# Attention heads behind later gate banks, one tile for both heads' chunk operands and state, other fill lengths, in a two-layer hybrid decoder trunk

## The chip, the cores and the metric

The kernel runs on one core of a Trainium2 chip. Its engines are told by the names that the profile uses: PE is TensorE (matrix products; PEld is its weight loads), DVE is VectorE, ACT is ScalarE, POOL is GpSimd, SP is SyncE, which issues the transfers of the weights. The metric is the device time of one run in microseconds (us), as the median of several runs. The profile is of one further execution, whose own time stands beside it.

## The reference

Two layers over 256 tokens of width 1024. Everything is float32. Cut to what matters here:

```python
h = rmsnorm(x, norm_mix[i]);  z = h @ w_in[i]
qa, ka, va, zr, gate_a, gate_r = split(z)         # attention, RWKV, two gates
oa = diff_attention(qa, ka, va, rel_bias, lam)    # 4 heads: softmax of two maps,
                                                  # W = P1 - lam * P2, W @ v
oa = rmsnorm(oa, attn_subln[i]) * (1 - lam_init)
y_attn = oa @ w_out_attn[i]

zs = zr + (token_shift(zr) - zr) * rwkv_mu[i]     # r, k, v, decay, a, g from it
def step(state, inp):                             # 8 heads, state 64 x 64
    sa = einsum('bhvk,bhk->bhv', state, a_t)      # a = -kk,  b = kk * a
    state = state * w_t + sa[..., None] * b_t + v_t[..., None] * k_t
    return state, einsum('bhvk,bhk->bhv', state, r_t)
yr = scan(step, 0, (r, decay, k, v, -kk, kk * a))
y_rwkv = ((groupnorm(yr) + bonus) * g) @ w_out_rwkv[i]

x = x + (sigmoid(gate_a) * y_attn + sigmoid(gate_r) * y_rwkv) @ w_out[i]
x = x + (silu(h2 @ w_ffn_gate[i]) * (h2 @ w_ffn_up[i])) @ w_ffn_down[i]
x = x + sigmoid(rmsnorm(x) @ w_ple_gate[i]) * (p[i] @ w_ple[i])
```

A last rmsnorm follows. The change touches `diff_attention` and `scan` only in how they are laid out in time and in memory.

## The kernel before

**The stream.** The weights of all the large products come from HBM in loads of 512 KB (8 blocks of 128x128). For each load ScalarE makes a rounded copy `wh` (L110) and VectorE the rest `wl = raw - wh` (L111). TensorE then does three products for each block, x with wh, the rest of x with wh, and x with wl (L128 to L130; L142, L144 and L166 to L168 are the same in other shapes). This stream goes through the whole program, and the smaller work is put between its products.

**What is set between.** In each layer the input projection, the attention, the gates and the attention's output projection are one generator, `main_g`: 14 banks for RWKV (`need(b)` forces one of them to be done), then q, k, v, then 8 gate banks. In its loop over the gate banks, head b's `scores` (two products into PSUM for each of two maps, additions of the bias on VectorE L469 and L470, maxima L472 and L473, exponentials, reciprocal L479, scaling by lambda L480) comes ahead of gate bank b, and `weighted` (transposes and product with v) behind it, for b from 0 to 3. The RWKV code is written as straight steps. Between them stand calls `fill(t)`, which let `main_g` advance by about t us of stream products, and t comes from a table, FP0 for layer 0 and FP1 for layer 1, by the name of the step (`pre`, `g0`, `tr`, `q0`, ...). Both tables are the same before. A scheduler then orders the instructions of each engine.

**The RWKV steps.** The 256 tokens are 4 chunks of 64. For a chunk c and a pair j of heads (e is 0 or 1, one head on each half of the 128 partitions; `half[e]` is the half, `quar` the quarters):

- The preparation makes `NK` (two operands side by side, L668 and L670) and `RA` (two side by side, L678 and L679), `RA` once for each e and each half of the pairs, with 64 partitions filled. L712 multiplies NK with RA: 8 products for each j. From the result ScalarE copies diagonal blocks to `AT` and `L2`, and VectorE masks one part into the free half of `RA` (L722) and one into `RK` (L723).
- `SV[e]` holds the state of the head on its half of the partitions and V on the other half; `UV[e]` the corrections and V. `NT` is NK transposed (L744).
- The diagonal blocks of 32x32 are inverted on VectorE (L765 to L797), scaled by per-partition columns into `ex` (L804, L805) and transposed into `D2` (L806), once for Ds and once for Dt. `blocks` (L818) does 64 products of 32x32 with Ds, a second call 64 with Dt.
- Then the chunks in turn: L843 forms Z of both heads (8 products of 128 rows, state and masked part in one sum), L854 solves with the diagonal blocks, L861 and L871 carry it to the second half, L876 forms the state's product, and L884 and L885 update `SV`, one operation for each e. Behind chunks 1 and 3 the outputs y are formed (L898, L903) and normalised.

The program begins with 11 products of a zero tile (`NWARM`, L233), before the first weights are there.

Of the kernel before, what the change touches and what calls it, by code (L numbers as in the profile page):

```python
# [25 lines left out]
NSLOT = 27  # L26
# [4 lines left out]
NWARM = 11  # L31

FP0 = dict(pre=1.29, g0=1.05, g=0.75, vt=0.39, rk=1.13, di=1.56, su=0.7, tr=0.36, q0=2.0, q1=1.6, z=0.95, w=1.15,
          w2=0.71, u=2.27, s=1.8, gn0=8.42, gn1=10.4, s8=1.06)
FP1 = dict(pre=1.29, g0=1.05, g=0.75, vt=0.39, rk=1.13, di=1.56, su=0.7, tr=0.36, q0=2.0, q1=1.6, z=0.95, w=1.15,
          w2=0.71, u=2.27, s=1.8, gn0=8.42, gn1=10.4, s8=1.06)
# [21 lines left out]
def trunk(ctx: ExitStack, tc: tile.TileContext, x_in, p_in, ws, par, lora, cst, fin, relb, onehot, out):  # L58
# [19 lines left out]
    def slot8(shape, dt=F32, s="s8"):  # L78
        return sp.tile(shape, dt, tag="s8", bufs=1, name=nm(s))
# [287 lines left out]
    def layer(l):  # L367
# [159 lines left out]
        def main_g():  # L527
# [19 lines left out]
            side = {}  # L547
            early["lam"] = attention_lambda()
            for b in range(8):
                if b < 4:  # L550
                    side[b] = scores(b)
                    yield 1.3
                gb = gate_bank(b)
                yield from gb
                if b < 4:
                    yield from weighted(b, side[b])
                if b == 3:
                    attention_norm()
                if b == 4:
                    yield from attention_out()  # L560
            oas = [(oh_[:, k], ol_[:, k]) for k in range(4)]
# [101 lines left out]
        RA = [[slot([P, 8, P], F32, "RA") for _ in range(2)] for _ in range(2)]  # L663
        NK = slot8([P, 16, 2, 64], F32, "NK")
# [3 lines left out]
        V.scalar_tensor_tensor(out=NK[:, :, 0], in0=pt16(nb), scalar=-0.5, in1=pt16(Pi), op0=ALU.mult, op1=ALU.mult)  # L668
        fill(fp['pre'])
        V.tensor_mul(NK[:, :, 1], pt16(kp), pt16(Pi))  # L670
        fill(fp['pre'])
        for jp in range(2):
            js = slice(2 * jp, 2 * jp + 2)
            for e in range(2):
                h = half[e]
                ra = RA[e][jp]
                A.copy(ra[h, :, 0:1], pt16(kn[:, js])[h, :, 0:1])
                V.tensor_mul(ra[h, :, 1:64], pt16(kn[:, js])[h, :, 1:64], pt16(Pd[:, js])[h, :, 0:63])  # L678
                V.tensor_mul(ra[h, :, 64:128], pt16(zr[:, js])[h], pt16(Pd[:, js])[h])  # L679
                fill(fp['pre'])  # L680
# [13 lines left out]
        RK = [slot([P, 16, 64], F32, "RK") for _ in range(2)]  # L694
# [8 lines left out]
        def mask4(h, lo):  # L703
            n = h.stop - h.start
            return mg[h, lo:lo + 64].unsqueeze(1).broadcast_to([n, 4, 64])

        for j in range(4):

            pgs = [psax(), psax()]
            for c in range(4):  # L710
                for e in range(2):
                    PE.matmul(pgs[e][:, c * P:(c + 1) * P], NK[half[e], 4 * j + c].rearrange("p a s -> p (a s)"),  # L712
                              RA[e][j // 2][half[e], 4 * (j % 2) + c], start=True, stop=True)
            for e in range(2):
                h, oh = half[e], half[1 - e]
                ra = RA[e][j // 2]
                pg = pgs[e]
                pg3 = pg.rearrange("p (i s) -> p i s", i=4)
                for b in range(2):
                    A.copy(AT[quar[2 * e + b], 4 * j:4 * j + 4], pg3[quar[b], :, quar[b]])  # L720
                A.copy(L2[quar[e], 4 * j:4 * j + 4, quar[e]], pg3[0:32, :, 32:64])
# [5 lines left out]
        SV = [slot([P, 16, 64], F32, "SV") for _ in range(2)]  # L727
        UV = [slot([P, 16, 64], F32, "UV") for _ in range(2)]
        NT = [slot([P, 8, P], F32, "NT") for _ in range(2)]
        for tb in range(2):  # L730
# [4 lines left out]
            for r in range(2):  # L735
                c = 2 * tb + r
                for e in range(2):
                    A.copy(SV[e][half[1 - e], c::4], pv4[half[r], :, e])
                    A.copy(UV[e][64:128, c::4], pv4[half[r], :, e])
            fill(fp['vt'])  # L740
        for i4 in range(4):
            pn = psax()
            for i in range(4):
                PE.transpose(pn[:, i * P:(i + 1) * P], NK[:, 4 * i4 + i].rearrange("p a s -> p (a s)"), ident)  # L744
            A.copy(NT[i4 // 2][:, 4 * (i4 % 2):4 * (i4 % 2) + 4], pn.rearrange("p (i v) -> p i v", i=4))
            fill(fp['vt'])
# [84 lines left out]
        for e in range(2):  # L831
            G.memset(SV[e][half[e], 0::4], 0.0)
# [5 lines left out]
        for c in range(4):  # L838
            ch = c // 2
            pz = psax()  # L840
            for j in range(4):
# [21 lines left out]
            for e in range(2):  # L863
                G.tensor_copy(UV[e][0:32, c::4], W1[quar[e]])
# [4 lines left out]
            V.tensor_copy(UV[0][32:64, c::4], four(pw)[quar[2]])  # L869
            A.copy(UV[1][32:64, c::4], four(pw)[quar[3]])  # L870
# [363 lines left out]
```

## Time and profile before

| | |
|---|---|
| median of 3 runs | 910.44 us (908.72 to 911.51) |
| profiled execution, its own time | 909.44 us |
| its span (first to last instruction) | 907.6 us |
| mean granted clock of TensorE | 0.994 |
| PE busy | 887.8 us, 98% of the span |
| PEld (weight loads beside it) | 800.3 us, 88% |
| DVE busy | 709.6 us, 78%, 1270 instructions |
| ACT busy | 515.8 us, 57% |
| POOL busy | 18.4 us, 2% |
| chain that ended last | PE 90%, DVE 6%, ACT 2% |
| HBM read | 147.25 MB, 165 GB/s over the span |

How to read it: the chain that ended last is followed back from the last instruction to what released each; its shares say which engine's work made up the time. A busy TensorE is not TensorE at its peak, since the ends of its products are modelled: the distance from one start to the next says more than the length of one. The granted clock is the share of full speed (2.4 GHz) that the engine was given; 0.5 is the lower level of 1.2 GHz. The other engines' shares are averages over the program; a stage of its own can look different, and the windows show that. Lines as L818 are lines of the kernel before.

### The profile page before, as it was taken

What the parts mean: (1) busy time and instruction counts of PE and PEld (TensorE: products, weight loads), DVE (VectorE), ACT (ScalarE), POOL (GpSimd) and SP (SyncE); (2) the same over time, 40 slices, a digit from 0 to 9 for tenths busy, and PEclk for the clock granted to TensorE, in tenths of its full rate; (3) what the DMA queues carried; (4) which work ended last, traced back from release to release, by engine and by line L of the source; (5) the groups of instructions that cost most, each with busy time, mean ns of one, the idle gap of its engine ahead of it and who ended that gap; (6) DMA issues with size and microseconds to landing.
All of it is one profiled execution on the core that took longest, in us unless ns stands there. A gap on an engine that the chain in (4) does not pass through costs nothing.

```text
span 907.6 us, 17784 instructions
## 1 busy us (share of the span) xinstructions
PE 887.8 (98%) x7011; PEld 800.3 (88%) x7011; DVE 709.6 (78%) x1270; ACT 515.8 (57%) x956; POOL 18.4 (2%) x59
## 2 busy tenths in 40 slices
PE   8999989999999999999999999999999999999996
PEld 7988879899988888889999997989989888888885
DVE  6659977688988888766785996768788888886666
ACT  6475665544555555545567564665465555554444
POOL 0000000100000000000001000000000000000000
PEclk9999999999999999999999999999999999999998
DMA  8563423445666666666554344333665666666661
GB/s 283 190 219 131 140 75 106 126 153 165 208 186 187 188 186 190 198 186 194 170 162 136 107 135 136 95 111 105 185 188 174 195 188 187 190 201 186 192 191 47
DMA packets 42540, 149.47 MB, mean 165 GB/s; under 512 B 4911, under 2 KB 6488, under 8 KB 42328
## 3 DMA queue, kind: packets, MB, share of 16 engines
q1 hardware_dynamic: 41896, 147.87, 53.6%
q8 instruction: 55, 0.90, 0.4%
q10 hardware_dynamic: 560, 0.46, 0.2%
q14 instruction: 29, 0.24, 0.1%
HBM read 147.25 MB, written 2.63 MB: 165 GB/s over the span
## 4 chain that ended last, share of the span: by engine, by line
PE 90%; DVE 6%; ACT 2%; issue 1%; DMA 1%; ACTq 0%; POOL 0%; DVEq 0%; POOLq 0%
PE mm L142 21%; PE mm L128 11%; PE mm L144 10%; PE mm L130 10%; PE mm L129 10%; PE ax L142 8%; PE ax L144 4%; DVE wl L111 2%; ACT wh L110 1%; PE mm L166 1%; PE ax L712 1%; PE mm L167 1%; PE mm L168 1%; PE ax L818 1%; PE ax L843 1%
## 5 line engine op out<-in xcount | busy, mean ns | idle before, releaser
L110 ACT CAST wh<-raw 128x1024 fp32r<-128x1024 f32 (+1 forms) x269 | 280.7, 1046 | 297.0 <-PE mm L142 100.6
L111 DVE TENSOR_TENSOR wl<-raw,wh 128x1024 fp32r<-128x1024 f32 (+1 forms) x269 | 327.3, 1219 | 105.4 <-ACT wh L110 103.9
L128 PE MATMUL mm<-x,wh 128*128 128x256 f32 x704 | 204.1, 290 | 2.1 <-ACT wh L110 1.7
L130 PE MATMUL mm<-x,wl 128*128 128x256 f32 x704 | 202.0, 288 | 0.6 <-DVE wl L111 0.5
L129 PE MATMUL mm<-x,wh 128*128 128x256 f32 x704 | 200.6, 285 | 0.0
L128 PEld LDWEIGHTS mm<-x,wh 128*128 128x128 f32 x704 | 135.0, 192 | 6.2 <-ACT wh L110 2.2
L130 PEld LDWEIGHTS mm<-x,wl 128*128 128x128 f32 x704 | 134.9, 192 | 4.2 <-DVE wl L111 1.6
L129 PEld LDWEIGHTS mm<-x,wh 128*128 128x128 f32 x704 | 135.0, 192 | 1.1 <-issue 0.2
L142 PE MATMUL mm<-f,wh 128*128 128x512 f32 x352 | 97.5, 395 | 0.0
L142 PE MATMUL mm<-x,wh 128*128 128x512 f32 x320 | 87.5, 395 | 0.0
L142 PE MATMUL ax<-x,wh 128*128 128x512 f32 x320 | 87.3, 394 | 0.0
L142 PEld LDWEIGHTS mm<-f,wh 128*128 128x128 f32 x352 | 59.7, 189 | 7.6
L144 PEld LDWEIGHTS mm<-f,wl 128*128 128x128 f32 x352 | 55.1, 189 | 8.1
L142 PEld LDWEIGHTS ax<-x,wh 128*128 128x128 f32 x320 | 54.7, 189 | 7.3
L142 PEld LDWEIGHTS mm<-x,wh 128*128 128x128 f32 x320 | 54.7, 189 | 7.3
L144 PE MATMUL mm<-f,wl 128*128 128x256 f32 x352 | 57.2, 280 | 0.0
L144 PEld LDWEIGHTS ax<-x,wl 128*128 128x128 f32 x320 | 49.1, 189 | 6.8
L144 PEld LDWEIGHTS mm<-x,wl 128*128 128x128 f32 x320 | 49.1, 189 | 6.8
L144 PE MATMUL ax<-x,wl 128*128 128x256 f32 x320 | 50.9, 281 | 0.0
L144 PE MATMUL mm<-x,wl 128*128 128x256 f32 x320 | 50.9, 281 | 0.0
L142 PE MATMUL mm<-m,wh 128*128 128x512 f32 x128 | 35.3, 396 | 0.0
L956 DVE TENSOR_TENSOR xs<-xs,mm 128x256 f32<-128x256 f32 x64 | 26.3, 416 | 9.3 <-PE mm L144 8.7
(293 smaller groups left out, 1385.1 us busy)
## 6 DMA issues: line engine op xcount, KB each, us to landing
raw<-ws SPq DMA_DIRECT2D x267, 512.0 KB, 3.6
lora<-lora SPq DMA_DIRECT2D x2, 768.0 KB, 5.6
vr<-vd SPq DMA_DIRECT2D x1, 1536.0 KB, 9.4
bias<-vr SPq DMA_DIRECT2D x1, 1024.0 KB
out<-y SPq DMA_DIRECT2D x3, 256.0 KB, 2.1
raw<-ws SPq DMA_DIRECT2D x2, 256.0 KB, 4.6
xs<-x_in SPq DMA_DIRECT2D x1, 512.0 KB
pi<-p_in SPq DMA_DIRECT2D x2, 256.0 KB, 3.8
```

Of the source, the lines that this page charges most:

```text
L110: A.copy(wh, raw)
L111: V.tensor_sub(wl, raw, wh.bitcast(F32))
L128: PE.matmul(dst, lh, rh, start=first, stop=False, **kw)
L129: PE.matmul(dst, lh, rl, start=False, stop=False, **kw)
L130: PE.matmul(dst, ll, rh, start=False, stop=last, **kw)
L142: PE.matmul(pm, wh[:, i * P:(i + 1) * P], src[k + i][2], start=k + i == 0, stop=False, skip_group_check=True)
L144: PE.matmul(pm[:, 0:T], wl[:, i * P:(i + 1) * P], src[k + i][0], start=False, stop=k + i == nk - 1, skip_group_check=True)
L166: PE.matmul(dst, x[0][:, tk], wh, start=first, stop=False, skip_group_check=True)
L167: PE.matmul(dst, x[1][:, tk], wh, start=False, stop=False, skip_group_check=True)
L168: PE.matmul(dst, x[0][:, tk], wl, start=False, stop=last, skip_group_check=True)
L712: PE.matmul(pgs[e][:, c * P:(c + 1) * P], NK[half[e], 4 * j + c].rearrange("p a s -> p (a s)"), RA[e][j // 2][half[e], 4 * (j % 2) + c], s ...
L956: V.tensor_add(xs[:, n], xs[:, n], pm)
```

## The change

Six things change together.

1. `LATE = (2, 1)`: head hd goes with gate bank hd + 2 in layer 0 and hd + 1 in layer 1, not with bank hd.
2. `RA` is one tile for both heads of a pair (128 partitions), no longer one for each e. To let it be read against both, `NK` gets a copy of its first operand as a third column block, and the view `nk[e]` orders the two blocks as (first, second) or (second, first) by e.
3. Both masked parts become one tile, `MK[e]`, made by one operation of 512 columns for each j and e instead of two of 256. `RK` goes.
4. The state is one tile `S` for both heads; `SV` and its copies of V go. Z becomes two groups of 64-row products, one with S (not in chunk 0) and one with MK and UV. The state's update is one operation for both e.
5. NK is transposed in halves: 64 transposes of 64 rows instead of 32 of 128. Of the four scalings into `ex` three go from VectorE to ScalarE.
6. The fill tables differ by layer and in several entries, and there are 15 products ahead of the first weights, no longer 11.

```diff
-NWARM = 11
+LATE = (2, 1)
+NWARM = 15
-FP0 = dict(pre=1.29, g0=1.05, ..., tr=0.36, q0=2.0, ..., z=0.95, w=1.15, ..., gn0=8.42, ...)
+FP0 = dict(pre=1.29, g0=1.36, ..., tr=0.26, q0=1.93, ..., z=0.78, w=1.43, ..., gn0=10.06, ...)
-FP1 = dict(pre=1.29, ..., g=0.75, ..., q0=2.0, ..., z=0.95, ..., w2=0.71, ..., s=1.8, gn0=8.42, ...)
+FP1 = dict(pre=2.06, ..., g=0.58, ..., q0=1.44, ..., z=0.1, ..., w2=0.6, ..., s=4.12, gn0=10.03, ...)
...
             for b in range(8):
-                if b < 4:
-                    side[b] = scores(b)
+                hd = b - LATE[l]
+                if 0 <= hd < 4:
+                    W_ = scores(hd)
...
+        A.copy(NK[0:64, :, 2], NK[0:64, :, 0])
+        nk = [NK[half[e], :, 1 - e:3 - e].rearrange("p i a s -> p i (a s)") for e in range(2)]
...
-            for e in range(2):
-                h = half[e]
-                ra = RA[e][jp]
-                A.copy(ra[h, :, 0:1], pt16(kn[:, js])[h, :, 0:1])
-                V.tensor_mul(ra[h, :, 1:64], pt16(kn[:, js])[h, :, 1:64], pt16(Pd[:, js])[h, :, 0:63])
-                V.tensor_mul(ra[h, :, 64:128], pt16(zr[:, js])[h], pt16(Pd[:, js])[h])
-                fill(fp['pre'])
+            ra = RA[jp]
+            A.copy(ra[:, :, 0:1], pt16(kn[:, js])[:, :, 0:1])
+            V.tensor_mul(ra[:, :, 1:64], pt16(kn[:, js])[:, :, 1:64], pt16(Pd[:, js])[:, :, 0:63])
+            fill(fp['pre'])
+            V.tensor_mul(ra[:, :, 64:128], pt16(zr[:, js]), pt16(Pd[:, js]))
+            fill(fp['pre'])
...
-                V.tensor_mul(ra[oh, 4 * (j % 2):4 * (j % 2) + 4, 0:64], pg3[64:128, :, 0:64], mask4(half[1], 0))
-                V.tensor_mul(RK[e][:, 4 * j:4 * j + 4], pg3[:, :, 64:128], mask4(slice(0, P), 64))
+                V.tensor_mul(MK[e][j // 2][:, 4 * (j % 2):4 * (j % 2) + 4], pg3, mg.unsqueeze(1).broadcast_to([P, 4, P]))
...
-                PE.transpose(pn[:, i * P:(i + 1) * P], NK[:, 4 * i4 + i].rearrange("p a s -> p (a s)"), ident)
+                for e in range(2):
+                    PE.transpose(pn[e][:, i * 64:(i + 1) * 64], nk[e][:, 8 * jp + i], ident[half[e], half[e]])
...
-            V.tensor_scalar_mul(ex[:, :, 0:16], src, p0)
-            V.tensor_scalar_mul(ex[:, :, 16:32], src, p1)
+            A.activation(ex[:, :, 16:32], src, AF.Copy, scale=p1)
+            if tile_ is Ds:
+                V.tensor_scalar_mul(ex[:, :, 0:16], src, p0)
+            else:
+                A.activation(ex[:, :, 0:16], src, AF.Copy, scale=p0)
...
+            if c > 0:
+                for j in range(4):
+                    for e in range(2):
+                        PE.matmul(four(pz)[half[e], j], RA[j // 2][half[e], 4 * (j % 2) + c, 0:64], S[half[e], 4 * j + c],
+                                  start=j == 0, stop=False, skip_group_check=True)
             for j in range(4):
                 for e in range(2):
-                    PE.matmul(four(pz)[half[e], j], RA[e][j // 2][:, 4 * (j % 2) + c, 0:64], SV[e][:, 4 * j + c],
-                              start=True, stop=True)
+                    PE.matmul(four(pz)[half[e], j], MK[e][j // 2][half[e], 4 * (j % 2) + c, 0:64], UV[e][half[e], 4 * j + c],
+                              start=c == 0 and j == 0, stop=j == 3, skip_group_check=True)
...
-                for e in range(2):
-                    h = half[e]
-                    if c > 0:
-                        V.tensor_add(S1[h], four(pS)[h], SV[e][h, c::4])
-                    V.tensor_mul(SV[e][h, c + 1::4], S1[h], PC[h, c::4].unsqueeze(2).broadcast_to([64, 4, 64]))
+                    V.tensor_add(S1, four(pS), S[:, c::4])
+                V.tensor_mul(S[:, c + 1::4], S1, PC[:, c::4].unsqueeze(2).broadcast_to([P, 4, 64]))
```

Three places show the order that comes of it. The first is VectorE in the preparation of layer 0, behind NK: the operations that make RA from kn, zr and the decays Pd. Before:

```order
L678 TENSOR_TENSOR RA_872<-kn_815,Pd_606 64x8x63
L679 TENSOR_TENSOR RA_872<-zr_147,Pd_606 64x8x64
L678 TENSOR_TENSOR RA_874<-kn_815,Pd_606 64x8x63
L679 TENSOR_TENSOR RA_874<-zr_147,Pd_606 64x8x64
L536 SCALAR_TENSOR_TENSOR q_149<-mm_880,bc_501 128x512
L111 TENSOR_TENSOR wl_953<-raw_951,wh_952 128x1024
L678 TENSOR_TENSOR RA_873<-kn_815,Pd_606 64x8x63
L679 TENSOR_TENSOR RA_873<-zr_147,Pd_606 64x8x64
L678 TENSOR_TENSOR RA_875<-kn_815,Pd_606 64x8x63
L679 TENSOR_TENSOR RA_875<-zr_147,Pd_606 64x8x64
L687 SCALAR_TENSOR_TENSOR rk_989<-zr_147,pr,kp_858 128x256 x4
L111 TENSOR_TENSOR wl_996<-raw_994,wh_995 128x1024
```

The same place after, with the same names, on VectorE too:

```order
L680 TENSOR_TENSOR RA_876<-kn_819,Pd_610 128x8x63
L682 TENSOR_TENSOR RA_876<-zr_151,Pd_610 128x8x64
L537 SCALAR_TENSOR_TENSOR q_153<-mm_882,bc_505 128x512
L112 TENSOR_TENSOR wl_953<-raw_951,wh_952 128x1024
L680 TENSOR_TENSOR RA_877<-kn_819,Pd_610 128x8x63
L682 TENSOR_TENSOR RA_877<-zr_151,Pd_610 128x8x64
```

Four pairs of 64 partitions have become two pairs of 128; a bank of q, a part of wl and the operation rk stand among and behind them as before.

The second is VectorE around the transposed diagonal blocks D of layer 0, which L818 (L819 after) needs. The scores' e and sm belong to head 0, bo is the bonus, DD the inverted blocks, ex their scaled form. Before:

```order
L470 TENSOR_TENSOR e_1357<-ax_1358,bias 128x128
L469 TENSOR_TENSOR e_1357<-ax_1359,bias 128x256
L470 TENSOR_TENSOR e_1357<-ax_1359,bias 128x128
L472 TENSOR_REDUCE sm_1368<-e_1357 128x2
L473 TENSOR_REDUCE sm_1368<-e_1357 128x2
L755 TENSOR_TENSOR bo_1251<-zv_148,ax_1384 128x512
L804 TENSOR_SCALAR ex_1389<-DD_1272,cs 128x16x16
L805 TENSOR_SCALAR ex_1389<-DD_1272,cs 128x16x16
L111 TENSOR_TENSOR wl_1397<-raw_1395,wh_1396 128x1024
L479 RECIPROCAL sm_1376<-sm_1371 128x4
L806 STREAM_TRANSPOSE D_262_1388<-ex_1389 128x16x32
```

After, on the same engine at the same place:

```order
L793 TENSOR_TENSOR p_248_1342<-DD_1270,u_246_1332 128x512
L753 TENSOR_TENSOR bo_1249<-zv_152,ax_1304 128x512
L795 TENSOR_REDUCE DD_1270<-p_248_1342 128x8x8
L804 TENSOR_SCALAR ex_1392<-DD_1270,cs 128x16x16
L112 TENSOR_TENSOR wl_1319<-raw_1317,wh_1318 128x1024
L807 STREAM_TRANSPOSE D_259_1391<-ex_1392 128x16x32
L807 STREAM_TRANSPOSE D_259_1391<-ex_1396 128x16x32
```

Head 0's scores have gone from here, one of the two scalings ahead of the transpose is left, and both transposes stand one behind the other; a part of wl stands ahead of the first in both.

The third is TensorE at Z of chunk 1 in layer 0 (SV, S: state; UV: corrections and V; mm: the stream). Before, the first two of the eight products of Z behind the scores of a head (k, q):

```order
L463 MATMUL ax_1776<-k_150,q_149 128x256
L463 MATMUL ax_1777<-k_150,q_149 128x256
L465 MATMUL ax_1776<-k_150,q_149 128x128
L465 MATMUL ax_1777<-k_150,q_149 128x128
L843 MATMUL ax_1802<-SV_1174,RA_872 64x64
L843 MATMUL ax_1802<-SV_1175,RA_874 64x64
```

Six more such rows follow, and then the stream. After, at the same place on TensorE:

```order
L129 MATMUL mm_1704<-x_116,wh_1612 128x256
L130 MATMUL mm_1704<-x_116,wh_1612 128x256
L844 MATMUL ax_1745<-S_1165,RA_876 64x64 x4
L844 MATMUL ax_1745<-S_1165,RA_877 64x64 x4
L848 MATMUL ax_1745<-UV_1166,MK_1022 64x64
L848 MATMUL ax_1745<-UV_1167,MK_1024 64x64
```

Six more rows with MK follow. Eight products of state and masked part in one have become eight with the state (two rows of four) and eight with the masked part; a head's scores stand ahead of them before and stream products after.

## Rows read from the trace of the kernel before

**Rows 1.** Waits of TensorE: engine, tile, line, releaser: us, times, longest

```profile
PE ax L818 <- DVE sm L480: 2.2, 1, 2.2
PE ax L818 <- DVE ex L805: 2.1, 1, 2.1
PE ax L818 <- issue: 0.8, 1, 0.8
PE ax L712 <- DVE RA L679: 0.7, 2, 0.5
PE mm L130 <- DVE wl L111: 0.5, 2, 0.3
PE ax L733 <- DVE RK L723: 0.3, 1, 0.3
```

**Rows 2.** Windows: busy us of PE, PEld, DVE, ACT, POOL, granted clock, DMA, GB/s

```profile
8.40:11.90 3.50, 3.50 (x19) 3.50 (x18) 3.35 (x7) 3.50 (x8) 0.00 (x0) 0.51 1.04 414
71.50:117.60 46.10, 42.72 (x306) 37.71 (x304) 44.97 (x83) 28.05 (x70) 0.94 (x3) 1.00 0.35 108
117.60:121.10 3.50, 3.42 (x135) 3.38 (x136) 3.24 (x6) 1.90 (x4) 0.44 (x2) 0.51 0.71 186
```

**Rows 3.** Groups of VectorE by shape: busy us, mean ns, idle before

```profile
L678 DVE TENSOR_TENSOR RA<-kn,Pd 64x504 f32<-64x504 f32 x8 | 5.4, 674 | 0.1
L722 DVE TENSOR_TENSOR RA<-ax,cs 64x256 f32<-64x256 f32 x16 | 6.8, 427 | 0.5
L653 DVE TENSOR_TENSOR kn<-kk,ax 128x512 f32<-128x512 f32 x4 | 2.6, 684 | 0.9 <-PE ax L651 0.9
```

**Rows 4.** Groups of VectorE, window 71.5 to 117.6: the scores' additions

```profile
L469 DVE TENSOR_TENSOR e<-ax,bias 128x256 f32<-128x256 f32 x2 | 0.8, 418 | 0.0
L470 DVE TENSOR_TENSOR e<-ax,bias 128x128 f32<-128x128 f32 x2 | 0.6, 284 | 0.0
```

**Rows 5.** TensorE in time, diagonal blocks, both layers: start, length, engine, line

```profile
117.68 1.93 PE L818 MATMUL ax<-D,BT 32*32 32x32 f32 x128 [2.15 <-DVE sm L480]
119.54 0.58 PE L130 MATMUL mm<-x,wl 128*128 128x256 f32 x1
...
549.05 1.28 PE L818 MATMUL ax<-D,BT 32*32 32x32 f32 x128 [2.07 <-DVE ex L805]
550.25 0.50 PE L167 MATMUL mm<-wh,x 128*128 128x512 f32 x1
```

**Rows 6.** TensorE in time, chunk 0 of layer 0, from 126.47

```profile
126.47 0.69 PE L843 MATMUL ax<-SV,RA 128*64 128x64 f32 x16
127.09 0.39 PE L128 MATMUL mm<-x,wh 128*128 128x256 f32 x1
127.31 0.28 PE L129 MATMUL mm<-x,wh 128*128 128x256 f32 x1
127.43 0.28 PE L130 MATMUL mm<-x,wl 128*128 128x256 f32 x1
...
129.01 0.68 PE L861 MATMUL ax<-W,L 64*64 64x64 f32 x8
129.61 0.38 PE L130 MATMUL mm<-x,wl 128*128 128x256 f32 x1
```

**Rows 7.** TensorE in time, preparation of layer 0: L712 and transposes

```profile
80.63 2.02 PE L712 MATMUL ax<-RA,NK 64*128 64x128 f32 x24 [0.19 <-DVE RA L679]
...
94.91 0.63 PE L744 MATMUL ax<-cs,NK 128*128 128x128 f32 x4
95.29 0.47 PE L166 MATMUL mm<-wh,x 128*128 128x512 f32 x1
```

**Rows 8.** TensorE in time, start of the program

```profile
7.32 0.38 PE L128 MATMUL mm<-x,wh 128*128 128x256 f32 x1 [1.71 <-ACT wh L110]
...
9.07 0.41 PE L128 MATMUL mm<-x,wh 128*128 128x256 f32 x1
9.29 0.41 PE L129 MATMUL mm<-x,wh 128*128 128x256 f32 x1
```

More of the change, by code (lines that the diff above doesn't have):

```diff
@@ L25 @@
 BPC = 8
-NSLOT = 27
+NSLOT = 26
 LEAD = 2
@@ L30 @@
 NFIRST = (8, 4)
-NWARM = 11
[L33 to L36, printed above, removed]
+LATE = (2, 1)
+NWARM = 15
+FP0 = dict(pre=1.29, g0=1.36, g=0.75, vt=0.39, rk=1.13, di=1.56, su=0.7, tr=0.26, q0=1.93, q1=1.6, z=0.78, w=1.43,
+           w2=0.71, u=2.27, s=1.8, gn0=10.06, gn1=10.4, s8=1.06)
+FP1 = dict(pre=2.06, g0=1.05, g=0.58, vt=0.39, rk=1.13, di=1.56, su=0.7, tr=0.36, q0=1.44, q1=1.6, z=0.1, w=1.15,
+           w2=0.6, u=2.27, s=4.12, gn0=10.03, gn1=10.4, s8=1.06)
 FP = (FP0, FP1)
@@ L76, in slot, with slot12 @@
         return sp.tile(shape, dt, tag="s", name=nm(s))
-    def slot8(shape, dt=F32, s="s8"):
-        return sp.tile(shape, dt, tag="s8", bufs=1, name=nm(s))
+    def slot12(shape, dt=F32, s="s12"):
+        return sp.tile(shape, dt, tag="s12", bufs=1, name=nm(s))
     def small(shape, dt=F32, tag="sm", bufs=8):
@@ L545, in main_g @@
                 A.activation(vt[:, tb], pv2[tb], AF.Copy, scale=stats()[0][:, tb:tb + 1])
-            side = {}
             early["lam"] = attention_lambda()
             for b in range(8):
-                if b < 4:
-                    side[b] = scores(b)
+                hd = b - LATE[l]
+                if 0 <= hd < 4:
+                    W_ = scores(hd)
                     yield 1.3
[L553 to L557, printed above, removed]
+                yield from gate_bank(b)
+                if 0 <= hd < 4:
+                    yield from weighted(hd, W_)
+                if hd == 3:
                     attention_norm()
-                if b == 4:
+                if hd == 4:
                     yield from attention_out()
+            if LATE[l] > 3:
+                yield from attention_out()
             oas = [(oh_[:, k], ol_[:, k]) for k in range(4)]
@@ L661, in pt16 @@
             return ap.rearrange("p j (c t) -> p (j c) t", c=4)
-        RA = [[slot([P, 8, P], F32, "RA") for _ in range(2)] for _ in range(2)]
-        NK = slot8([P, 16, 2, 64], F32, "NK")
+        RA = [slot([P, 8, P], F32, "RA") for _ in range(2)]
+        NK = slot12([P, 16, 3, 64], F32, "NK")
         nb = slot([P, 4, T], F32, "nb")
@@ L693, in layer @@
         AT = slot([P, 16, 32], F32, "AT")
-        RK = [slot([P, 16, 64], F32, "RK") for _ in range(2)]
+        MK = [[slot([P, 8, P], F32, "MK") for _ in range(2)] for _ in range(2)]
         L2 = slot([P, 16, 64], F32, "L2")
@@ L737, in layer @@
                 for e in range(2):
-                    A.copy(SV[e][half[1 - e], c::4], pv4[half[r], :, e])
-                    A.copy(UV[e][64:128, c::4], pv4[half[r], :, e])
+                    A.copy(UV[e][half[e], c::4], pv4[half[r], :, e])
             fill(fp['vt'])
-        for i4 in range(4):
-            pn = psax()
-            for i in range(4):
-                PE.transpose(pn[:, i * P:(i + 1) * P], NK[:, 4 * i4 + i].rearrange("p a s -> p (a s)"), ident)
-            A.copy(NT[i4 // 2][:, 4 * (i4 % 2):4 * (i4 % 2) + 4], pn.rearrange("p (i v) -> p i v", i=4))
-            fill(fp['vt'])
+        for jp in range(2):
+            pn = [psax(), psax()]
+            for i in range(8):
+                for e in range(2):
+                    PE.transpose(pn[e][:, i * 64:(i + 1) * 64], nk[e][:, 8 * jp + i], ident[half[e], half[e]])
+            for e in range(2):
+                A.copy(NT[jp][:, :, half[e]], pn[e].rearrange("p (i v) -> p i v", i=8))
+                fill(fp['vt'])
         bo = slot([P, 4, T], F32, "bo")
@@ L868, in layer @@
                           skip_group_check=True)
-            V.tensor_copy(UV[0][32:64, c::4], four(pw)[quar[2]])
-            A.copy(UV[1][32:64, c::4], four(pw)[quar[3]])
+            V.tensor_copy(UV[0][quar[3], c::4], four(pw)[quar[2]])
+            A.copy(UV[1][quar[1], c::4], four(pw)[quar[3]])
             fill(fp['u'])
@@ L897, in layer @@
                         if cc > 0:
-                            PE.matmul(four(py[e])[half[cc % 2], j], RA[e][j // 2][half[e], 4 * (j % 2) + cc, 64:128],
-                                      SV[e][half[e], 4 * j + cc], start=j == 0, stop=False, skip_group_check=True)
+                            PE.matmul(four(py[e])[half[cc % 2], j], RA[j // 2][half[e], 4 * (j % 2) + cc, 64:128],
+                                      S[half[e], 4 * j + cc], start=j == 0, stop=False, skip_group_check=True)
             for j in range(4):
@@ L902, in layer @@
                     for cc in (c - 1, c):
-                        PE.matmul(four(py[e])[half[cc % 2], j], RK[e][:, 4 * j + cc], UV[e][:, 4 * j + cc],
+                        PE.matmul(four(py[e])[half[cc % 2], j], MK[e][j // 2][:, 4 * (j % 2) + cc, 64:128], UV[e][:, 4 * j + cc],
                                   start=cc == 0 and j == 0, stop=j == 3, skip_group_check=True)
```

23 lines of the change are left out of this document (8 added, 15 removed).

## Prediction

> **What bounds the kernel now.** I read the waits of TensorE first [rows 1]: the engine that does the stream of weight products is nearly always at work, so a microsecond is won only where it waits, runs at the lower clock, or does work that can go. The two longest waits are the same place in each layer: the first products with the inverted diagonal blocks (L818) wait 2.2 and 2.1 us for a VectorE operand. The profile names a small softmax operation (L480) for the first; by time it is the transpose L806 queued just before it, which ends as L480 starts. Then come small waits for RA, for the low weight parts (wl) and for RK, 0.7, 0.5 and 0.3, and one of 0.8 that no engine ends ("issue").
>
> The windows come next [rows 2]. From 71.5 to 117.6, the preparation of the chunks in layer 0, VectorE is busy 44.97 of 46.1 us: there it, and not TensorE, sets the pace, and the L818 wait is its last arrears. Right behind it, from 117.6 to 121.1, the granted clock is 0.51, the 1.2 GHz level. At the start of the program, from 8.4 to 11.9, it is 0.51 again. So a wait can be followed by a second cost; layer 1 shows that it need not be: behind the same wait its 128 products take 1.20 us, those of layer 0 1.86 [rows 5].
>
> **The change part by part, layer 0.** VectorE's work ahead of L806 shrinks. RA is now made for both heads of a pair by one operation of 128 partitions instead of two of 64: 8 operations of 0.674 us [rows 3] become 4. A 64-partition operation costs what a 128-partition one of the same columns does (L678 0.674 at 504 columns, L653 0.684 at 512), so half goes: 8 x 0.674 - 4 x 0.684 = 2.7 us. The two masks L722 and its twin L723, 8 each per layer, of 256 columns at 0.427, become 8 of 512 columns, by L653 (which reads PSUM too) 0.684 each: 16 x 0.427 - 8 x 0.684 = 1.4 us. Head 0's scores go behind L818, with two additions of 0.42, two of 0.28 [rows 4] and two reductions: at least 0.8 + 0.6 = 1.4. So the transposed block comes at least 5.5 us earlier in VectorE's own time. TensorE needs it earlier too: by its wait of 2.2, and by what it no longer does or waits for before it. That is the small waits in this layer (about 1), some eight stream products that the order now has behind L818 (8 x 0.12 = 1) and the scores' products (less than 1): 3 in all, so 5.2 against 5.5 or more, with the reductions and the ex scalings moved to ScalarE as margin. Term: -2.2 for the wait, and -1.5 for the three small ones of both layers (RK and RA are made by fewer operations; wl stands less often behind them).
>
> With the wait the low clock after it should go. At the lower level the 128 products of L818 take 1.86 us from their start to the next stream product (117.68 to 119.54), at the higher 1.20 (549.05 to 550.25) [rows 5]; the seven stream products behind them are 0.22 apart [rows 8] against 0.12 [rows 6]: 0.66 + 7 x 0.10 = 1.4. Term: -1.4, between 0 (clock stays low) and that.
>
> **Layer 1.** No scores stand ahead of L818 there; RA and masks give 4.1 us of VectorE. The larger fill `pre` only moves stream products from behind the RA operations to ahead of them, while VectorE works. Wait 2.1 against 4.1: term -2.1. If it did not hold, the wait stays, 0.
>
> **Start.** Four more warm-up products fill about half the idle 1.71 us ahead of the first real one at 7.32 [rows 8] (at 0.22 each); that one waits for its weights, so it comes no later. What can be won is the low clock from 8.4 to 11.9: 3.5 us at 0.22 for what takes 0.12 a product, so 16 products x 0.10, less what the new supply of weights may hold back: -1.4, with 0 as the other end. Layer 0's fall came behind 2.15 us of idleness [rows 5] and layer 1's 2.07 brought none, so the shorter gap is a fair chance and no certainty.
>
> **What is added.** Z of a chunk was one product per head of 128 rows (state and masked part stacked, L843), 8 per chunk. It is now, in chunks 1 to 3, 8 for the state and 8 for the masked part, each of 64 rows. One product of the program is two PE instructions in the trace (8 listed in the order are x16). So 2 layers x 3 chunks x 8 = 48 products or 96 instructions are added, and the 128 of L843 lose half their rows. Price: L843 takes 0.62 from its start to the next stream product, 0.19 of it for entering and leaving (127.09 to 127.31 is 0.10 over the usual 0.12, and as much, nearly, at the entry), so 0.43 / 16 = 0.027 an instruction [rows 6]. L861, single 64x64 products with no partner in the other half of the columns, takes 0.60: 0.41 / 8 = 0.051. The new ones alternate between the two row halves and column halves, so they look like L843. I take 0.027: 96 x 0.027 = +2.6, and nothing for the masked ones; the upper end is 0.051, +4.9 and 128 x 0.024 = +3.1. Nothing shows a product of both halves on the diagonal as such; L712, which alternates row halves alone with 128 columns moving, takes 2.02 / 24 = 0.084 [rows 7].
>
> The 32 transposes of NK (128x128, four in 94.91 to 95.29, so 0.095 each [rows 7]) become 64 of 64 rows. The lower end is half the price each, 0; the upper the full price, 32 x 0.095 = +3.0. L712 says 0.084 with twice the moving columns, so I take 0.06: 64 x 0.06 - 3.0 = +0.8. The Trainium skill ("TensorE: Matmul & The Clock Gate", section "LDWEIGHTS (loading the stationary operand)") speaks against this edit: a weight load goes by the columns of the stationary operand and not by its rows, and these halves still have 128 columns. By it alone the sum would take +3.0; no run here shows a half transposed.
>
> Visits to the small groups fall from 98 to 94 in the order, at 0.19: -0.8. The state's update becomes one VectorE operation for both heads instead of two, the copies of V into the state tile (SV) go, as do four GpSimd fills: all beside the stream, cost and gain nothing. Moved there: three of four ex scalings to ScalarE, in front of L806's inputs, where they queue behind a weight cast; softmax of head 0 into the chunk loop, ahead of the state updates on VectorE. The smallest fill between two chunk steps stays at 4 stream products (0.48 us). I add +0.5 for waits that appear so, between 0 and 2.0. The weight loads on SP's queue keep their order, since the gate banks do; only heads move among them.
>
> **Sum.** -2.2 - 1.5 - 1.4 - 2.1 - 1.4 - 0.8 = -9.4; +2.6 + 0.8 + 0.5 = +3.9; together -5.5. On the profiled execution's own 909.44 that is 903.9. It stands 1.0 below the median of the three runs, 910.44, so I forecast 904.9. The likeliest case's own range is 902 to 908.
>
> **Rivals.** (1) Slower: the 64-row products do not run side by side. Place: Z of each chunk. With a price p an instruction the Z products cost 96p + 128(p - 0.027); the other terms leave 9.4 - 0.8 - 0.5 = 8.1 to spend, so from p = 0.052 the kernel is slower. At L861's 0.051 the sum is -0.1, 910.3; at L712's 0.084 it is 8.1 + 7.3 - 8.1 = +7.3, 917.7. For it: L861. Against: L843 has the same column halves. Chance 0.13, of which 0.05 above the break-even.
> (2) The clock does not rise: the start's fall stays (+1.4), another comes in the preparation or at the transposes in a row (+1.4), and half the small waits stay (+0.8). -5.5 + 3.6 = -1.9: 908.5. For it: two falls in the trace that four products may not cure. Against: L744's transposes among the stream show no fall in their window [rows 2]. Chance 0.17. The same page's "Part 4: PE-mode transpose" says that products in transpose mode do not bring the full clock; the 64 halves, in rows of 16, would then be such a place, and that is in this chance.
> (3) More: the 0.84 of issue between the parts of L818 goes with the wait before it, and neither transposes nor waits cost. -9.4 - 0.8 + 2.6 = -7.6: 902.8. Chance 0.10.
> That the order does not do what it says: L818's wait stays in one layer, 2.2 less gain, 907.1; this lies within the forecast's 0.60.
>
> **Chances.** 0.3% is 2.7 us, about what can be told from no change: under 907.7 is faster, over 913.2 slower. Faster: 0.58 of the forecast's 0.60, 0.06 of (2), 0.10 of (3): 0.74. Same: 0.02 + 0.09 + 0.08 of (1) = 0.19. Slower: 0.05 of (1) and 0.02 of (2). Range 901 to 909.5: it leaves out (1) and a little on either side.
>
> **What would show it.** Right: no wait over 0.5 at L818's counterpart (L819) in either layer, clock 1.00 behind it and from 8.4 to 11.9, Z's two groups together near 1.05 us from entry to exit, and four half transposes near 0.24. Wrong: Z's groups at 1.4 or more (rival 1), a 0.5 in the granted clock anywhere but at the end (rival 2), or L818 still waiting for a transpose, which would mean that VectorE was late for another reason than the operations counted here.

## The result, and the profile after

The changed kernel takes 896.61 us (median of 4 runs, 895.75 to 897.39) against 909.58 for the kernel before beside it (4 runs): a ratio of 0.9862, 95% interval 0.9848 to 0.9875. So 12 to 13 us went, where 5.5 were forecast, and the time lies under the range. The direction was right, the size was not.

The waits of TensorE in the changed kernel that bear on the argument (engine, tile, line, releaser: us, times, longest), the counterpart of [rows 1]:

```profile
PE mm L131 <- DVE wl L112: 0.8, 2, 0.5
PE mm L129 <- ACT wh L111: 0.7, 1, 0.7
PE ax L819 <- issue: 0.7, 2, 0.4
PE ax L712 <- DVE RA L682: 0.5, 1, 0.5
PE ax L859 <- issue: 0.4, 1, 0.4
PE ax L881 <- ACT UV L875: 0.4, 1, 0.4
```

L819 is the L818 of before: its two waits of 2.2 and 2.1 are gone, and no wait for VectorE at that line is left. Of the three small waits, that for RA went from 0.7 to 0.5, that for RK is gone, and that for wl rose from 0.5 to 0.8. The windows that answer to [rows 2] (busy us of PE, PEld, DVE, ACT, POOL, granted clock, DMA share, GB/s):

```profile
8.40:11.90 3.50, 3.50 (x31) 3.48 (x30) 3.34 (x6) 3.50 (x8) 0.00 (x0) 1.00 1.03 410
69.80:108.90 39.10, 38.07 (x306) 34.16 (x304) 38.44 (x62) 25.69 (x56) 0.77 (x3) 1.00 0.44 128
108.90:112.40 3.50, 3.50 (x148) 3.45 (x148) 1.92 (x3) 1.25 (x2) 0.00 (x0) 1.00 0.68 180
```

The preparation of layer 0 now runs from 69.8 to 108.9, 39.1 us where it took 46.1, and VectorE's work in it fell from 44.97 to 38.44: the stage shrank by 7.0, VectorE's work by 6.5. The clock is 1.00 where it was 0.51, at the start and behind the diagonal blocks. Their products, in time (start, length, engine, line), the counterpart of [rows 5]:

```profile
108.91 1.29 PE L819 MATMUL ax<-D,BT 32*32 32x32 f32 x128
110.12 0.38 PE L129 MATMUL mm<-x,wh 128*128 128x256 f32 x1
...
539.61 1.29 PE L819 MATMUL ax<-D,BT 32*32 32x32 f32 x128
540.83 0.50 PE L167 MATMUL mm<-wh,x 128*128 128x512 f32 x1
```

1.21 and 1.22 us from their start to the next stream product, in both layers, and no wait in front.

Two groups came out otherwise than the prediction had them. First the kernel before again, two sets of L712 in layer 0 that its rows did not show, each with the stream product that follows:

```profile
88.70 1.13 PE L712 MATMUL ax<-RA,NK 64*128 64x128 f32 x8
89.76 0.39 PE L130 MATMUL mm<-x,wl 128*128 128x256 f32 x1
90.43 1.19 PE L712 MATMUL ax<-RA,NK 64*128 64x128 f32 x16
91.55 0.39 PE L128 MATMUL mm<-x,wh 128*128 128x256 f32 x1
```

Eight instructions of one half of the partitions take 1.06 us, sixteen by turns 1.12. The 2.02 / 24 = 0.084 of [rows 7] was a mean of these two kinds. In the changed kernel all sets are by turns, though some take up to 1.6 us with their first steps and a wait; the shortest kind, and the 32 half transposes of one group:

```profile
80.68 1.16 PE L712 MATMUL ax<-RA,NK 64*128 64x128 f32 x16
81.77 0.39 PE L129 MATMUL mm<-x,wh 128*128 128x256 f32 x1
...
91.70 1.21 PE L741 MATMUL ax<-cs,NK 64*128 64x64 f32 x32
92.85 0.50 PE L167 MATMUL mm<-wh,x 128*128 128x512 f32 x1
```

Sixteen in 1.09, and 32 half transposes in 1.15, 0.036 each, where full ones started 0.109 apart (the 0.095 of the prediction divides a set of four up to the next stream product, whose last step is shorter). Last, Z of chunk 1 in layer 0, state and then masked part:

```profile
128.20 0.68 PE L844 MATMUL ax<-S,RA 64*64 64x64 f32 x16
128.72 0.63 PE L848 MATMUL ax<-UV,MK 64*64 64x64 f32 x16
129.28 0.39 PE L131 MATMUL mm<-x,wl 128*128 128x256 f32 x1
```

0.52 and 0.56, together 1.08 from entry to exit; the prediction said 1.05.

### The profile page after: what moved, and what is told of

It is laid out like the page before. It is cut to its first block, busy times and chain, and to the rows that moved or that the text cites. A ratio compares the mean times of both kernels' runs of the same rounds, so it can differ in the third digit from the quotient of the medians.

```text
span 895.6 us, 17981 instructions
## 1 busy us (share of the span) xinstructions
PE 881.0 (98%) x7143; PEld 796.2 (89%) x7143; DVE 694.4 (78%) x1230; ACT 515.0 (58%) x944; POOL 16.9 (2%) x55
## 4 chain that ended last, share of the span: by engine, by line
PE 94%; DVE 3%; DMA 1%; ACT 1%; issue 1%; ACTq 0%; POOL 0%; POOLq 0%; DVEq 0%
PE mm L143 20%; PE mm L129 12%; PE mm L131 11%; PE mm L130 11%; PE mm L145 10%; PE ax L143 8%; PE ax L145 4%; PE mm L167 1%; PE mm L169 1%; PE mm L168 1%; PE ax L712 1%; DVE wl L112 1%; DMA pi<-p_in 1%; PE ax L819 1%; PE ax L859 1%
```

## Where the 12 us are

Each product's start to the next one's start, added up by line over the whole profiled execution, with a group's waits and the steps into and out of it counted to the group, and set against the terms of the sum (the profiled spans are 907.6 and 895.6):

| place | forecast | in the two profiles |
|---|---|---|
| waits ahead of L818, both layers | -4.3 | -4.3 |
| L712: its products, with what they wait for | -0.7 | -3.9 |
| transposes of NK, and entering them | +0.8 | -2.1 |
| products of V's transposes (they waited for RK) | -0.3 | -0.6 |
| y from the masked part (L903) | 0 | -1.0 |
| start: low clock and first product | -1.4 | -1.7 |
| behind L818: low clock | -1.4 | -1.3 |
| Z, with entering and leaving | +2.6 | +1.4 |
| new waits ahead of two steps in layer 1 (L859, L881) | +0.5 | +1.5 |

The rest (fewer visits, small waits for wl) is below 1 us. A second measure, used below, is the distance from the first transpose of KR, at the start of the preparation, to the first product of L818 or its counterpart: 46.8 us in layer 0 and 50.0 in layer 1 before, 39.7 and 48.9 after. In layer 1 it hides most of what was won, because the new FP1 puts more of the stream into it: 289 stream products, where the kernel before has 266 (layer 0: 187 and 195). With the fill tables of before, in a run told below, there are 265 of them, and the distance is 44.2. The windows of layer 1, first before, then after, then with the fill tables of before (columns as above):

```profile
499.10:549.00 49.90, 47.30 (x371) 43.95 (x370) 48.44 (x84) 28.79 (x65) 0.63 (x2) 1.00 0.42 122
490.70:539.60 48.90, 48.90 (x410) 45.72 (x409) 46.41 (x71) 30.50 (x61) 0.32 (x1) 1.00 0.49 144
490.90:535.10 44.20, 44.20 (x388) 41.47 (x387) 43.04 (x69) 28.17 (x59) 0.32 (x1) 1.00 0.45 128
```

So at the same amount of stream the preparation of layer 1 shrank by 5.8, and VectorE's work in it by 5.4, much as in layer 0.

## The experiments

Times are medians. The kernel before stood beside each: 908.62 for the first four, 908.55 for the next four, 908.33 for the four after these, 910.16 for the last two. The changed kernel, taken once more, is the last of the third group.

**Warm-up alone.** The kernel before with

```diff
-NWARM = 11
+NWARM = 15
```

> The kernel before with 15 warm-up products instead of 11 and nothing else. Theory (the low clock at the start is what these four products take away): the granted clock is 1.00 from 8.4 to 11.9, 16 products come 0.12 and not 0.22 apart, and the first real product comes up to 0.3 earlier: -1.4 to -1.8 us, about 908 on a median of 909.6. Rival (the clock's rise at the start in the changed kernel came from another order of the first loads and casts): the low clock stays, 0 us.

908.98 us, ratio 1.0001 (0.9991 to 1.0010). The theory is wrong, though its profile looks like a hit: that one execution is 1.6 us earlier behind the start and has no low clock there. Over 12 timed runs the mean granted clock is 0.9947, over 23 of the kernel before 0.9948. Of the sixteen profiles, one of four with 11 products has the low clock at the start, and none of twelve with 15. So 15 may yet take away what one execution in a few has; that would be about 0.4 us in the mean, an estimate from 1.7 us in one of four, and the interval cannot show it. The forecast's -1.4 is out.

**The reverse.** The changed kernel with `NWARM = 11`.

> The changed kernel with 11 warm-up products. Theory (the low clock at the start is a draw of one execution: the kernel before with 11 and heads late had none in its profile, and with 15 alone the median did not move): 0 us within 0.5, and a mean granted clock over the runs within 0.0007 of the changed kernel's 0.9973. Rival (15 are what keeps the clock up here): +1 to +1.6 us and a mean clock lower by 0.001 to 0.002.

895.64 us, ratio 0.9863 (0.9850 to 0.9877), mean clock 0.9970: 0.7 below the changed kernel run again (896.31, below), a little outside the 0.5 that the theory gave, and far from the rival's +1 to +1.6: 15 are not what keeps the clock up here. With 11 products the same window (columns as above) is

```profile
8.40:11.90 3.50, 3.50 (x31) 3.50 (x31) 3.35 (x6) 3.50 (x7) 0.00 (x0) 1.00 1.04 412
```

**Heads late, alone.** The kernel before with the new loop over the gate banks and `LATE = (2, 1)`.

> The kernel before with the heads behind the gate banks (two in layer 0, one in layer 1) and nothing else. Theory (the wait at L818 in layer 0 is VectorE's arrears, and head 0's scores are 2.8 us of them: additions 1.4, reductions 1.1, the rest 0.3): the wait of 2.15 there falls below 0.5, the low clock behind it goes with it, together -3 to -3.6 us; layer 1's wait of 2.07 stays, since no scores stand ahead of it there. The products of L712 stay in the order that they had, so their 11.0 us stay. About 906.3. Rival (the wait comes from RA and the masks, which stay): 0 to -1 us and a granted clock of 0.51 again.

908.29 us, ratio 0.9995 (0.9985 to 1.0006). The theory falls. The wait at the diagonal blocks (L821 here) stays in both layers, 2.1 us each:

```profile
PE ax L821 <- DVE ex L808: 4.2, 2, 2.1
```

The distance to L818 in layer 0 fell from 46.8 to 45.1, since TensorE had the scores' products and some stream less to do ahead of it; VectorE was as late as before in relation to it. The granted clock falls behind the wait in layer 0 again, as the rival said.

**Heads in place.** The changed kernel with `LATE = (0, 0)`.

> The changed kernel with head b again at gate bank b in both layers. Theory (heads late alone gave nothing on the kernel before, since RA and the masks held VectorE up; here 2.8 us of scores come back on VectorE against a margin of 2.6): a wait of 0 to 0.7 at L819 in layer 0, none in layer 1, +0 to +1.5 us. Rival (the heads' place is what freed VectorE): a wait of 2 us in layer 0 and a low clock behind it, +2 to +4.

899.10 us, ratio 0.9899 (0.9884 to 0.9914), 2.8 above the changed kernel. Neither as said: no wait for VectorE at L819's first set (one of 1.5 for ScalarE at its second), and the distance grows by 1.0 in layer 0 and by nothing in layer 1. The rest comes between the diagonal blocks of layer 0 and the preparation of layer 1, 1.9 longer. So the heads' place is worth 2.8 here and nothing on the kernel before.

**Old fill tables.** The changed kernel with FP0 and FP1 of before.

> The changed kernel with the two equal fill tables of the kernel before. Theory (the waits at the diagonal blocks went because VectorE has less to do; the tables only place the stream): the transposed blocks end 2.6 and 2.3 us before they are needed in the changed kernel, so no wait over 0.5 there, and the time is 0 to +1.5 us over the changed kernel's. Rival (the tables set it: the larger fill ahead of L712 in layer 1 and the others give VectorE its time): the wait of about 2 us comes back in layer 1, and some in layer 0, +2 to +4 us.

897.78 us, ratio 0.9886 (0.9872 to 0.9899), 1.5 above the changed kernel, and no wait for VectorE at L819: theory right, at its upper end. The waits ahead of L859 and L881 are absent here, so they came with the new tables.

**Halves not by turns.** The changed kernel with, at L712,

```diff
-            for c in range(4):
-                for e in range(2):
+            for e in range(2):
+                for c in range(4):
```

> The changed kernel with e outside c at L712: four products of one half of the partitions, then four of the other, instead of by turns; the same work in all. Theory (two 64-row products of different halves run side by side, two of the same half do not; this gave the 3.3 us at L712 that the prediction did not have): 0.111 an instruction as in the one-half groups of the kernel before, so a set of 16 takes 1.8 instead of 1.1: 8 sets, +5 to +6.5 us. Rival (L712 is faster because both heads read one RA tile, or since it waits less for it): 0, within 1 us.

898.44 us, ratio 0.9886 (0.9870 to 0.9902): about +2, the right sign and too small. A set in layer 0:

```profile
80.41 1.71 PE L712 MATMUL ax<-RA,NK 64*128 64x128 f32 x16
82.05 0.39 PE L129 MATMUL mm<-x,wh 128*128 128x256 f32 x1
```

1.64 and not 1.8: where the two fours meet, the trace shows products of the other half between those of the first. In all L712 takes 3.4 us longer, and the distance to L818 grows by 1.0 and 1.8.

**Half transposes not by turns.** The same edit at L741 (`for e` outside `for i`).

> The changed kernel with e outside i at the half transposes: eight of one half, then eight of the other; the same work. Theory (the halves run side by side when they alternate): without it each takes what its 64 moving columns take, about 0.06, and the two sets of 32 per layer take 2.0 us instead of 1.14 each time: +1.5 to 2 us. Rival A (a half transpose is bound by loading 128 columns of weights, as its full one, 0.109): +4 to 5 us. Rival B (the halves were cheap by their 64 columns alone, and not by lying side by side): 0.

896.09 us, ratio 0.9861 (0.9845 to 0.9877): no difference in time. A group:

```profile
91.59 1.64 PE L741 MATMUL ax<-cs,NK 64*128 64x64 f32 x32
93.15 0.50 PE L167 MATMUL mm<-wh,x 128*128 128x512 f32 x1
```

1.56 for 1.15, which is +0.8 in two layers, too little to show in these times. Where one half stands alone the starts are 0.062 to 0.064 apart, far from 0.109: rival A is out. By turns, two of different halves take those 0.062 together, as the theory said. But the edit left 18 of the 32 in such pairs, and there is one group of 32 in each layer and not two, so the theory's +1.5 to 2 was too much for this edit. What the turns do is to halve the price once more, which rival B leaves out; whether the fewer rows or the fewer moving columns made the half alone cheaper than a full one is not shown.

**VectorE's load back.** The changed kernel with its operations cut as before, in the new tiles:

```diff
-            V.tensor_mul(ra[:, :, 1:64], ...)
-            fill(fp['pre'])
-            V.tensor_mul(ra[:, :, 64:128], ...)
-            fill(fp['pre'])
+            for h in half:
+                V.tensor_mul(ra[h, :, 1:64], ...)
+                V.tensor_mul(ra[h, :, 64:128], ...)
+                fill(fp['pre'])
...
-                V.tensor_mul(MK[e][j // 2][:, ...], pg3, mg...)
+                for lo in (0, 64):
+                    V.tensor_mul(MK[e][j // 2][:, ..., lo:lo + 64], pg3[:, :, lo:lo + 64], mg[:, lo:lo + 64]...)
```

> The changed kernel with VectorE's operations cut as before, in the new tiles: RA by 64 partitions (16 operations for 8), each mask in two of 256 columns (32 for 16). The same values. In the order that comes of it, half of L712's products stand again in runs of one half. Theory (less work on VectorE is what took away the waits at the diagonal blocks): 2.7 + 1.4 us a layer come back against margins of 2.6 and 2.3, so waits of 1 to 2 us at L819 in both layers, 0.5 more for each of about four sets of L712 that are not by turns, and small waits ahead of L712: +4 to +7 us. Rival (the layout and the order on TensorE gave the gain): only the sets of L712, +1 to +2 us.

905.10 us, ratio 0.9965 (0.9952 to 0.9978): +8.8, above what the theory said and far above the rival. The distance to L818 becomes 45.3 and 52.6 (+5.6 and +3.6). But the waits of TensorE (its longest for VectorE in that stage) are small:

```profile
PE ax L712 <- DVE MK L721: 1.5, 1, 1.5
PE ax L821 <- DVE D L809: 0.8, 1, 0.8
PE ax L712 <- DVE RA L682: 0.5, 1, 0.5
```

Where VectorE is late, TensorE waits inside L712, or its products stand in another order; at L821 only 0.8 is seen. L712 with its waits takes 15.3 us in this profile and 9.8 in the changed kernel's, 5.6 of the 8.3 between the two. In layer 0 VectorE has 2.7 us more to do and the distance is 5.6 longer: VectorE is busy 41.35 of 45.29 us there, and 38.70 of 39.73 in the changed kernel, so its added work alone does not make up the longer stage.

**RA alone, masks alone.** The two halves of that edit.

> The changed kernel with RA alone made by 64 partitions again (16 operations for 8, +2.7 us of VectorE in each layer). In the order of it the products of L712 stand in runs of one half in layer 0 (three of four sets), and by turns in layer 1. Theory A (in the preparation each microsecond of VectorE's work is one of time, whatever TensorE does meanwhile): +5 to +6 us, about as much from layer 1 as from layer 0. Theory B (what counts is the order of the halves): +1.5 to +2 us, all of it from layer 0.

> The changed kernel with each mask alone made in two operations of 256 columns (32 for 16, +1.4 us of VectorE in each layer). L712 stays by turns in both layers. Theory A (each microsecond of VectorE there is one of time): +2.5 to +3 us. Theory B (the order of the halves): 0 to +0.5. A third (the margin of 2.6 and 2.3 us at the diagonal blocks takes it in): 0.

RA alone: 902.23 us, ratio 0.9935 (0.9922 to 0.9949), +5.9; theory A in its sum. The distance grows by 4.1 in layer 0, where L712 loses its turns, and by 2.0 in layer 1, where it keeps them. There it is a plain wait in the middle of a set:

```profile
517.71 1.38 PE L712 MATMUL ax<-RA,NK 64*128 64x128 f32 x18
520.63 1.16 PE L712 MATMUL ax<-RA,NK 64*128 64x128 f32 x14 [1.54 <-DVE MK L720]
521.71 0.38 PE L129 MATMUL mm<-x,wh 128*128 128x256 f32 x1
```

1.54 us for a mask, which on VectorE stands behind rk, a bank of q and two parts of wl. Masks alone: 898.42 us, ratio 0.9890 (0.9876 to 0.9903), +2.1, near A by the time. But the distances are 40.0 and 48.9, so the preparation took them in, as the third theory said; in the profile 1.5 are lost, 0.9 of it in layer 1 behind L818. Two waits of a stream product stand there, behind the first diagonal blocks of each layer, that neither profile of the changed kernel has:

```profile
PE mm L129 <- issue: 1.6, 2, 1.0
```

What they wait for the profile does not name; it stays open.

**Scalings alone.** The kernel before with three of four `ex` on ScalarE, as in the change.

> The kernel before with three of the four scalings ex on ScalarE and nothing else: 1.1 us less of VectorE in each layer, 0.4 of it ahead of the first transposed block and the rest behind it. Theory A: the wait at L818 falls by 0.4 in each layer and the second set comes earlier, -0.8 to -2 us. Rival (ScalarE has a weight cast in front, and the wait is only handed on): 0.

910.12 us, ratio 1.0020 (1.0006 to 1.0034): slower by a little. The two waits at L818's counterpart stay, 2.3 and 2.1. This part of the change gains nothing by itself.

**The changed kernel again.**

> The changed kernel once more beside these, so that they stand on one chip. All theories: the ratio of the first time, 0.986 of the kernel before, within 0.002; a mean clock of 0.997.

896.31 us, ratio 0.9868 (0.9853 to 0.9883), mean clock 0.9968.

**Still less on VectorE.** The changed kernel with

```diff
-            V.scalar_tensor_tensor(out=rk[:, j], in0=zr[:, j], scalar=pl[:, ...], in1=kp[:, j],
-                                   op0=ALU.mult, op1=ALU.mult)
+            A.activation(rk[:, j], zr[:, j], AF.Copy, scale=pl[:, ...])
+        G.tensor_mul(rk, rk, kp)
```

and the same with `V.tensor_mul(rk, rk, kp)`.

> The changed kernel with rk (4 VectorE operations of 0.48 us in each layer, 1.9 in all, behind RA and ahead of the masks) made by ScalarE (scaling) and GpSimd (product). Theory A (VectorE still sets the pace in the preparation: it is busy 36.8 of 37.4 us there in layer 0): -1 to -2 us, nearly all from layer 0. Theory C (in the changed kernel VectorE is early enough, by the margin of 2.6 and 2.3 us at the diagonal blocks, and TensorE sets the pace): 0 within 0.5. Slower by up to 2 if ScalarE's four scalings come in front of weight casts, or GpSimd's product slows VectorE.

> The changed kernel with rk scaled by ScalarE and multiplied by VectorE in one operation of 1024 columns (1.22 us by the rows of that shape, for four of 0.48): 0.7 us less on VectorE in each layer, 2.2 more on ScalarE, nothing on GpSimd. Theory A: -0.5 to -1. Theory C: 0. If ScalarE's place in front of the casts is what counts, as slow as the one with GpSimd.

On GpSimd: 900.59 us, ratio 0.9898 (0.9880 to 0.9915), slower than the changed kernel by 2.7 us by the ratios and 4.3 by the medians, more than any of the theories gave. (They differ since the kernel before took 910.16 beside this run and 908.33 beside the changed kernel.) GpSimd's product and the VectorE operation that runs beside it:

```profile
74.02 3.35 POOL L691 TENSOR_TENSOR rk<-rk,kp 128x1024 f32<-128x1024 f32 x1 [27.00 <-DVE q L537]
```

```profile
75.03 3.42 DVE L674 TENSOR_TENSOR NK<-kp,Pi 128x1024 f32<-128x1024 f32 x1
```

VectorE's 128x1024 product takes 3.42 where it takes 1.22 in the changed kernel; it ends 1.08 us after GpSimd's product. The operation ahead of it on VectorE, also 128x1024, ran beside the first microsecond of GpSimd's and took its usual 1.22:

```profile
73.89 1.22 DVE L670 SCALAR_TENSOR_TENSOR NK<-nb,Pi 128x1024 f32<-128x1024 f32 x1
```

TensorE waits for the RA behind them, and behind that wait, from 81.7 on, the granted clock is 0.50, the lower level, which is part of the loss:

```profile
PE ax L712 <- DVE RA L682: 2.7, 1, 2.7
```

With VectorE's own product: 894.84 us, ratio 0.9834 (0.9818 to 0.9851), 1.5 below the changed kernel by the medians, 3 by the ratios, and the fastest of all here; both are above the 0.5 to 1 of theory A. The distance falls from 39.7 to 39.3 in layer 0 and stays 48.9 in layer 1. So in layer 0 VectorE still sets some of the pace, 0.4 us of it by the distance; where the rest of the gain lies is not shown. In layer 1 the distance is 48.9 in the changed kernel, with heads in place, with masks split and here: TensorE sets it.

## Why the prediction was wrong

Direction, place and the waits at L818 were right; the sum was 6.5 us short of the profiles and 7.5 of the first medians. By its own steps:

- **The step that failed**: "So the transposed block comes at least 5.5 us earlier in VectorE's own time", and then "Term: -2.2 for the wait". The first half holds as far as it can be read (RA 0.68 and masks 0.683 an operation, as priced). The second took the relief to be worth only the waits that the profile showed at L818, -2.2 and -2.1, and those did go. But with the load of RA and masks put back, 8.2 us of VectorE's work as priced (2.7 + 1.4 in each layer), the kernel loses 8.8 us and waits only 0.8 at the diagonal blocks: the delay stands ahead of and inside L712, as waits and as lost turns. The next point is the same miss seen on TensorE. It is no law of one for one: RA alone costs 5.9, masks alone 2.1, and the masks left the preparation's length as it was.
- **L712, held at no change.** Its price of 0.084 in the upper bound was a mean of 0.13 (sets of one half, 1.06 / 8) and 0.07 (by turns, 1.12 / 16). The kernel before had four sets with one half apart, and the prediction did not look at which half followed which. In the two profiles 3.9 us went there, with the waits; breaking the turns alone costs 2.
- **Half transposes: +0.8 forecast, -2.1 in the profiles.** 0.036 each, not 0.06, against full ones of 0.109, not 0.095; and they are entered less often. The rule of the Trainium skill ("TensorE: Matmul & The Clock Gate", "LDWEIGHTS (loading the stationary operand)"), by which the sum would have taken +3.0, is not borne out here: with the same 128 columns of weights the halves start 0.062 to 0.064 apart even where one half follows itself.
- **Start, -1.4**: nothing that the timed runs can show. The low clock in the profile of before was one execution's, and the experiments with 11 and 15 products show no difference in time. That the two profiles differ by 1.7 there is chance, and not a hit. The rows at hand could not tell it from a cause; the range of the term had 0 as its end, the sum took the other.
- **Low clock behind L818, -1.4**: the profiles show -1.3 (0.65 in the products, 7 x 0.10 in the stream), and the mean clock rises from 0.9948 to between 0.9968 and 0.9973 in the timed runs. The warm-up does not do it. In the sixteen profiles the granted clock falls to the lower level seven times ahead of the program's end, each time at the end of a wait of TensorE of 1.5 to 2.8 us or within 2 us behind it. Seven profiles, all of the changed kernel or its variants, have no wait over 1.2 us, and no such fall. A wait need not bring one: with the warm-up alone 2.15 and 2.08 brought none. So the waits that went are the likely reason; no run isolates it.
- **Z, +2.6**: right mechanism and price, 0.52 for the 16 added instructions of a chunk. The entry and exit are shared by both groups, so less is left, +1.4. Rival 1 (no products side by side) is out.
- **Rival 2** (a low clock at transposes in a row): the window from 69.8 to 108.9, with the group at 91.7, is at 1.00. Against it here.
- **Heads late**: counted as part of VectorE's relief. By itself 0, in the changed kernel 2.8, of which 1.9 behind the diagonal blocks of layer 0, where the prediction named only a cost.
- **Small waits, -1.5**: 1.3 of them are left. **y from the masked part**, held at no change: -1.0.

The new Z, the one tile for the state, y from MK, and half transposes against full ones were not run alone; what is said of their worth rests on the two profiles.

## What to carry to other kernels

Where an engine is busy 97% of a stage, do not price what is taken off it by the waits alone that another engine shows at the end: a late operand can appear as a worse order or a slower set further up. The share by itself proves nothing either. In the changed kernel VectorE is busy 38.44 of 39.1 us of layer 0's preparation, and with the masks' 1.4 us more the distance grew by 0.2. Putting the work back is what tells. Split a mean price before it is used, by which neighbours the instructions had. A low clock that one profile shows is no term until several executions show it.

## What the runs showed of the hardware

- Products of 64 rows on alternating halves of the partitions: 16 instructions in 1.09 us; four products of one half and then four of the other, 1.64.
- Transposes of 64 rows: 0.062 to 0.064 us from start to start on one half alone, the same for two by turns on both halves; full ones 0.109.
- A GpSimd product of 128x1024 (3.35 us) beside a VectorE product of the same shape: that takes 3.42 instead of 1.22 us and ends 1.08 after GpSimd's. Another VectorE operation, beside the first microsecond of it, kept its 1.22.
- In 23 executions of the kernel before the mean granted clock lies between 0.992 and 0.998 and the time between 907.01 and 911.51 us; on the whole the lower clocks have the longer times.
